# Long convolution of a conformer block: a timed schedule replaced by plain loops, with taps added on the matmul bank

## The chip, the cores and the metric

The kernel runs on one core of one Trainium2 chip. The metric is the device time of one execution in microseconds, as the median of several runs. Inside the core, TensorE (PE) does matmuls, VectorE (DVE), ScalarE (ACT) and GpSimdE (POOL) do elementwise work, and SyncE (SP) issues the weight loads. Each engine works through its own queue in the order in which the instructions were built into the program.

## The reference, cut to what matters

The whole program is a chain of blocks on a 256 x 1024 activation: a mixing layer, a cross-attention, a feed-forward layer, this conformer block, a feed-forward layer, a sparse attention and a last feed-forward layer. Only the conformer block is touched. The input h is a normalized x.

```python
def conformer_conv_module(h, w_in, b_in, w_dw, b_dw, ln_g, ln_b, w_out):
    a, g = jnp.split(h @ w_in + b_in, 2, axis=-1)
    u = a * jax.nn.sigmoid(g)
    u = lax.conv_general_dilated(          # 31 taps, depthwise, causal
        u, w_dw[:, None, :].astype(u.dtype), window_strides=(1,),
        padding=[(CONV_WIDTH - 1, 0)], dimension_numbers=('NWC', 'WIO', 'NWC'),
        feature_group_count=D_MODEL) + b_dw
    ...                                     # layer norm over the channels
    u = jax.nn.silu(uf).astype(h.dtype)
    return u @ w_out
```

## The kernel before, in words

Channels lie on the 128 partitions and the 256 positions along the free dimension, so the 1024 channels make eight tiles, m = 0 to 7. For each tile, the block first forms the product of w_in with x (`product_of`): two blocks of 128 channels in one bank, the value and the gate. For m = 1 and 2 the weights are split in a high and a low half (`mm3`, three matmuls for each of 16 pairs, L215 to L217); for m = 3 to 7 raw weights meet `cxg` (L990). DVE multiplies the bank by a broadcast of 1/rms (`rb`, L971 and L973), ACT applies tanh and a bias (L975, L976; below "the pair"), and DVE combines them (L977) to u(m), the tile `cu`.

The convolution adds 31 shifted copies of u(m), each scaled by a weight for each channel. Three engines share them. PE takes `CONV_PE[m]` of the shortest shifts as matmuls with a diagonal matrix `cdg` made by ACT (L1042, L1048), into a bank `bt`. POOL takes the `CONV_GP[m]` longest: ACT writes each scaled copy to a `cpr` tile, of which there are four (L1028), and POOL adds them in `cyp` (L1029). DVE takes the rest with one instruction per tap, (u x weight) + y, in the SBUF tile `cy` (L1015). Then DVE adds the bank to cy (L1057), and POOL or DVE adds cyp (L1059). The mean of tile 0 is broadcast (`cb`) and taken off every tile as a first guess of the mean. ACT squares y, and PE sums y and its square over the channels into `zb` (L1077). Behind the last tile follow the statistics, the normalization, silu, the split into two halves `yy`, and the product with c_out.

The order of the work is set by the table `CONF_AT`: `timed` starts each unit ("in" for the gated product, "pe", "gp", "dv", "fin", and "x") at its listed time and lets it take turns. What this gives each engine is a fixed queue. The unit "x" runs the generator `rest`, which multiplies the residual x by its gain and 1/rms in place (L438, eight instructions, behind a broadcast `bc_x1`).

Weights are loaded through a ring of four raw tiles `wraw` (L181). ACT casts a half (L198), and the rest is a subtraction (L200) on DVE, or for c_out chunks above the first on POOL.

Of the kernel before, what the change touches and what calls it, by code (L numbers as in the profile page):

```python
# [103 lines left out]
class Net:  # L104
# [825 lines left out]
    def conformer(self, first, pool):  # L930
# [6 lines left out]
        rb = zb = cb = None  # L937
        bt, yp = [None] * KT, [None] * KT
        have = set()

        def need(*keys):
            while not have.issuperset(keys):
                yield
# [13 lines left out]
        for m in range(KT):
            nc.vector.tensor_scalar(xg[:, m, :], self.x[:, m, :], gg[:, m : m + 1], None, op0=ALU.mult)

        def inp(m):  # L960
            nonlocal rb, zb
            b = b0
            if m:
                b, pb = product_of(m)
            yield
# [12 lines left out]
            have.add(f"u{m}")  # L978

        def product_of(m):  # L980
            nonlocal rb, zb
            w = self.chunk("c_in", m, **({"stop": "c_out"} if m < KT - 1 else {"room": 2}))
            pb = self.bank()
            b = [pb[:, 0:S], pb[:, S : 2 * S]]
            raw = [r.rearrange("p (k c) -> p k c", k=4) for r in w] if m >= CONV_N3 else None

            def product(i, k):
                c = slice(i * P, i * P + P)
                if raw:
                    nc.tensor.matmul(b[i][:, 0:S], raw[k // 4][:, k % 4, c], xg[:, k, :],  # L990
                                     start=(k == 0), stop=(k == KT - 1))
                else:
                    self.mm3(b[i][:, 0:S], w[k][:, :, c], self.xx[:, k], k == 0, k == KT - 1)

            for i in range(2):
                for k in range(KT):
                    product(i, k)
                if m == 1 and i == 0:
                    rb = self.bcast(r12, "x")
                    zb = self.zbank(2 * NT)  # L1000
            return b, pb

        def dv(m):
            yield from need(f"u{m}")
            y, u = ys[m], us[m]
            if m > 2:
                yield from need("c")
                nc.scalar.activation(y, cb, AF.Identity, bias=self.col("c_b", m), scale=-1.0)  # L1010
                nc.vector.scalar_tensor_tensor(y, u, tap(m, 0), y, op0=ALU.mult, op1=ALU.add)
            else:
                nc.vector.tensor_scalar(y, u, tap(m, 0), self.col("c_b", m), op0=ALU.mult, op1=ALU.add)
            for t in range(1 + CONV_PE[m], W - CONV_GP[m]):
                nc.vector.scalar_tensor_tensor(y[:, t:S], u[:, 0 : S - t], tap(m, t), y[:, t:S], op0=ALU.mult, op1=ALU.add)  # L1015
                if t % 4 == 0:
                    yield
            have.add(f"d{m}")
            yield
# [622 lines left out]
```

## Time and profile before

| | |
|---|---|
| median of 3 runs | 1132.01 us (1129.48 to 1132.69) |
| profiled execution | 1132.2 us |
| span of its trace | 1130.4 us |
| PE busy | 1070.3 us (95%) |
| DVE busy | 827.4 us (73%) |
| ACT busy | 638.2 us (56%) |
| POOL busy | 195.4 us (17%) |
| granted TensorE clock, mean | 0.974 |

The span runs from the first to the last instruction of the trace; busy time is the time in which an engine had an instruction at work. These are means over stages with different limits. In the timelines a row gives the start in us, the length of the group, the engine, the source line, the operation with output and inputs, and the count; in square brackets stands how long the engine was idle before it and what ended that. Instructions of one engine overlap by some 0.08 us, so a group's length divided by its count is the spacing. [...]

### The profile page before, as it was taken

The numbers are of one execution on the slowest core, as the hardware profiler recorded it, in microseconds if no ns is written. First come the engines' busy times: TensorE is split into PE (matmuls) and PEld (weight loads), VectorE is DVE, ScalarE is ACT, GpSimd is POOL, SyncE is SP. The second block draws the span as 40 slices with busy tenths as digits, with TensorE's granted clock in tenths as the row PEclk, the third lists the DMA queues.
The fourth block names the chain that finished last, engine by engine and source line by source line (L and its number), as shares of the span: only waits on it lengthen the run. The fifth ranks groups of instructions, "written<-read, shape, count | busy, mean of one in ns | idle before, by whom it ended". The sixth has DMA issues, their size and how long they took to land.

```text
span 1130.4 us, 19501 instructions
## 1 busy us (share of the span) xinstructions
PE 1070.3 (95%) x7282; PEld 984.6 (87%) x7282; DVE 827.4 (73%) x1654; ACT 638.2 (56%) x1231; POOL 195.4 (17%) x388
## 2 busy tenths in 40 slices
...
GB/s 233 220 167 158 127 147 155 128 135 191 187 193 178 219 169 71 65 85 93 75 113 176 190 191 183 223 173 189 95 112 189 18 76 149 188 190 192 179 208 31
DMA packets 52439, 171.38 MB, mean 152 GB/s; under 512 B 8440, under 2 KB 10360, under 8 KB 52344
## 3 DMA queue, kind: packets, MB, share of 16 engines
...
HBM read 169.07 MB, written 1.05 MB: 150 GB/s over the span
## 4 chain that ended last, share of the span: by engine, by line
PE 79%; DVE 12%; ACT 3%; issue 2%; DMA 2%; POOL 1%; SPq 0%; POOLq 0%; ACTq 0%; DVEq 0%
PE pb L223 28%; PE pb L224 14%; PE pb L215 9%; PE pb L216 9%; PE pb L217 9%; DVE cy L1015 5%; DMA wraw<-in_w_in_dram 1%; ACT wpr L198 1%; DVE wpr L200 1%; DVE xx L278 1%; DVE xres L438 1%; DVE xres L395 1%; PE bh L1254 1%; DMA wraw<-in_n_out_dram 1%; PE zb L376 1%
## 5 line engine op out<-in xcount | busy, mean ns | idle before, releaser
L200 DVE TENSOR_TENSOR wpr<-wraw,wpr 128x1024 fp32r<-128x1024 f32 (+1 forms) x298 | 361.1, 1214 | 178.7 <-ACT wpr L198 176.4
L198 ACT CAST wpr<-wraw 128x1024 fp32r<-128x1024 f32 (+1 forms) x304 | 313.4, 1033 | 203.1 <-PE pb L224 96.0
L223 PE MATMUL pb<-xx,wpr 128*128 128x512 f32 x840 | 294.3, 393 | 0.0
L224 PE MATMUL pb<-xx,wpr 128*128 128x256 f32 x840 | 235.5, 280 | 0.0
L223 PEld LDWEIGHTS pb<-xx,wpr 128*128 128x128 f32 x840 | 158.5, 189 | 34.0
L223 PE MATMUL pb<-fhs,wpr 128*128 128x512 f32 x528 | 186.0, 394 | 0.0
L224 PEld LDWEIGHTS pb<-xx,wpr 128*128 128x128 f32 x840 | 158.5, 189 | 0.0
L224 PE MATMUL pb<-fhs,wpr 128*128 128x256 f32 x528 | 147.3, 279 | 0.0
L215 PE MATMUL pb<-xx,wpr 128*128 128x256 f32 x456 | 129.7, 287 | 7.7 <-ACT xx L277 7.7
L216 PE MATMUL pb<-xx,wpr 128*128 128x256 f32 x456 | 130.4, 287 | 2.5 <-DVE xx L278 2.5
L217 PE MATMUL pb<-xx,wpr 128*128 128x256 f32 x456 | 128.9, 283 | 0.0
L223 PEld LDWEIGHTS pb<-fhs,wpr 128*128 128x128 f32 x528 | 99.0, 187 | 23.0
L224 PEld LDWEIGHTS pb<-fhs,wpr 128*128 128x128 f32 x528 | 99.0, 188 | 0.0
L215 PEld LDWEIGHTS pb<-xx,wpr 128*128 128x128 f32 x456 | 86.7, 192 | 9.4 <-ACT xx L277 8.0
L216 PEld LDWEIGHTS pb<-xx,wpr 128*128 128x128 f32 x456 | 87.3, 191 | 4.2 <-DVE xx L278 3.3
L217 PEld LDWEIGHTS pb<-xx,wpr 128*128 128x128 f32 x456 | 87.4, 192 | 0.0
L215 PE MATMUL pb<-yy,wpr 128*128 128x256 f32 x256 | 73.1, 288 | 2.3 <-ACT yy L282 2.3
L216 PE MATMUL pb<-yy,wpr 128*128 128x256 f32 x256 | 72.7, 284 | 0.0
L217 PE MATMUL pb<-yy,wpr 128*128 128x256 f32 x256 | 72.6, 284 | 0.0
L1015 DVE SCALAR_TENSOR_TENSOR cy<-cu,cwh,cy 128x238 f32<-128x238 f32 (+18 forms) x117 | 71.6, 669 | 0.1
L869 ACT COPY ft<-pb 128x256 f32<-128x256 f32 x105 | 38.5, 368 | 55.2 <-PE pb L224 55.2
L1029 POOL TENSOR_TENSOR cyp<-cyp,cpr 128x229 f32<-128x229 f32 (+11 forms) x70 | 59.9, 860 | 26.1 <-ACT cpr L1028 22.0
...
## 6 DMA issues: line engine op xcount, KB each, us to landing
wraw<-in_up_dram SPq DMA_DIRECT2D x44, 512.0 KB, 4.0
wraw<-in_up2a_dram SPq DMA_DIRECT2D x44, 512.0 KB, 4.4
wraw<-in_up2b_dram SPq DMA_DIRECT2D x44, 512.0 KB, 3.8
wraw<-in_w_in_dram SPq DMA_DIRECT2D x22, 512.0 KB, 4.6
wraw<-in_n_in_dram SPq DMA_DIRECT2D x20, 512.0 KB, 4.1
wraw<-in_wkv_dram SPq DMA_DIRECT2D x16, 512.0 KB, 3.7
wraw<-in_dn_dram SPq DMA_DIRECT2D x16, 512.0 KB, 4.4
wraw<-in_c_in_dram SPq DMA_DIRECT2D x16, 512.0 KB, 4.1
```

Source lines behind the costliest of these rows:

```text
L198: self.nc.scalar.copy(hi, raws[j])
L200: lane.tensor_tensor(lo, raws[j], hi.bitcast(F32), op=ALU.subtract)
L215: mm(out, left[:, 0], right[:, 0], start=start, stop=False, skip_group_check=True)
L216: mm(out, left[:, 0], right[:, 1], start=False, stop=False, skip_group_check=True)
L217: mm(out, left[:, 1], right[:, 0], start=False, stop=stop, skip_group_check=True)
L223: mm(out, left[:, 0], right, start=start, stop=False, skip_group_check=True)
L224: mm(out[:, 0], left[:, 1], right[:, 0], start=False, stop=stop, skip_group_check=True)
L278: nc.vector.scalar_tensor_tensor(lo, src, g, hi.bitcast(F32), op0=ALU.mult, op1=ALU.subtract)
L376: self.nc.tensor.matmul(zb[:, tt : tt + 1], src[:, tt * P : tt * P + P], self.ones, start=(src is acc), stop=(src is sq))
L869: nc.scalar.copy(t, b[:, 1])
L1015: nc.vector.scalar_tensor_tensor(y[:, t:S], u[:, 0 : S - t], tap(m, t), y[:, t:S], op0=ALU.mult, op1=ALU.add)
L1029: nc.gpsimd.tensor_tensor(y[:, t:S], y[:, t:S], pr[:, t:S], op=ALU.add)
```

## The change

The schedule table is gone. A plain loop issues, tile by tile, the product of the next tile, its gate, its diagonal matmuls and its POOL taps, and then the DVE taps and the end of the current tile. DVE's taps add in place on the bank `bt` behind the diagonal matmuls, and one DVE add then brings the bank to `cy`. POOL adds straight on `cy`, which ACT has set up with the bias (and tap 0 for m up to 2; for the others tap 0 is POOL's). There is no `cyp`. The numbers of taps change: PE 45 to 38 in all, DVE 117 and the eight of tap 0 to 113, POOL 70 adds to 94. The diagonal tiles have 12 buffers where they had 24. The subtractions for c_out are all DVE's. The second step of `rest`, the rescaling of x, is called behind the product with c_out.

```diff
-CONV_PE = [4, 1, 1, 4, 1, 15, 11, 8]
-CONV_GP = [8, 10, 10, 10, 14, 6, 9, 11]
+CONV_PE = [4, 3, 3, 3, 4, 5, 6, 10]
+CONV_GP = [13, 13, 12, 12, 12, 11, 9, 7]
...
-        lane = self.nc.gpsimd if name == "c_out" and idx > 0 else self.nc.vector
-        lane.tensor_tensor(lo, raws[j], hi.bitcast(F32), op=ALU.subtract)
+        self.nc.vector.tensor_tensor(lo, raws[j], hi.bitcast(F32), op=ALU.subtract)
...
+        def pe(m):
+            bt[m] = self.bank("bt")
+            n = CONV_PE[m]
+            for t in range(1, n + 1):
+                d = pool.tile([P, P], F32, name="cdg", tag="cdg", bufs=12)
+                nc.scalar.mul(d, self.ident, tap(m, t))
+                nc.tensor.matmul(bt[m][:, t:S], d, us[m][:, 0 : S - t], start=(t == 1), stop=(t == n))
 
         def dv(m):
...
+            b, u = bt[m], us[m]
+            for t in range(1 + CONV_PE[m], W - CONV_GP[m]):
+                nc.vector.scalar_tensor_tensor(b[:, t:S], u[:, 0 : S - t], tap(m, t), b[:, t:S], op0=ALU.mult, op1=ALU.add)
+
+        def gp(m):
             y, u = ys[m], us[m]
+            shifts = list(range(W - CONV_GP[m], W))
             if m > 2:
...
+                shifts = [0] + shifts
             else:
...
+                nc.scalar.activation(y, u, AF.Identity, bias=self.col("c_b", m), scale=tap(m, 0))
+            for t in shifts:
                 pr = pool.tile([P, S], F32, name="cpr", tag="cpr", bufs=4)
                 nc.scalar.mul(pr[:, t:S], u[:, 0 : S - t], tap(m, t))
                 nc.gpsimd.tensor_tensor(y[:, t:S], y[:, t:S], pr[:, t:S], op=ALU.add)
...
-        timed([(u[0], u[1], kinds[u[2]](*u[3:])) for u in CONF_AT])
+        gated(0, None)
+        pe(0)
+        gp(0)
+        next(rest)
+        for m in range(KT):
+            if m + 1 < KT:
+                gated(m + 1, product(m + 1))
+                pe(m + 1)
+                gp(m + 1)
+            if m == 0:
+                for k in range(KT):
+                    nc.vector.tensor_scalar(xg[:, k, :], self.x[:, k, :], gg[:, k : k + 1], None, op0=ALU.mult)
+            dv(m)
+            fin(m)
...
         acc = self.proj("c_out")
+        next(rest)
```

The numbers of the lines shift, too: the DVE tap L1015 becomes L979, the add of the bank L1057 becomes L997, the product by rb L973 becomes L959, u's L977 becomes L963, the diagonal matmul L1048 becomes L974, the raw product L990 becomes L948, the sums L1077 become L1010, the copies L1028 become L991, the rescaling L438 becomes L425, and the cast L198 becomes L186.

The builder orders the instructions of each engine. On DVE, in the piece where tile 1 ends and tile 2 goes on, these rows stood before (`cy1`, `cy2` are the sums of tiles 1 and 2, `bt` a bank, `cag` the gate's tile):

```order
L1015 SCALAR_TENSOR_TENSOR cy1_5160<-cu1_5152,cwh_5168,cy1_5160 128x238
L1015 SCALAR_TENSOR_TENSOR cy2_5161<-cu2_5153,cwh_5168,cy2_5161 128x253
L1015 SCALAR_TENSOR_TENSOR cy1_5160<-cu1_5152,cwh_5168,cy1_5160 128x237
L1015 SCALAR_TENSOR_TENSOR cy2_5161<-cu2_5153,cwh_5168,cy2_5161 128x252
L1015 SCALAR_TENSOR_TENSOR cy1_5160<-cu1_5152,cwh_5168,cy1_5160 128x236
L1015 SCALAR_TENSOR_TENSOR cy2_5161<-cu2_5153,cwh_5168,cy2_5161 128x251
L1057 TENSOR_TENSOR cy1_5160<-bt_5378,cy1_5160 128x255
L1015 SCALAR_TENSOR_TENSOR cy2_5161<-cu2_5153,cwh_5168,cy2_5161 128x250
L973 TENSOR_TENSOR cag_5475<-pb_5411,bc_x_5208 128x512
L1015 SCALAR_TENSOR_TENSOR cy2_5161<-cu2_5153,cwh_5168,cy2_5161 128x249
```

Now a single tile's taps follow one another; here is a piece of tile 0 (`bt_5185` its bank, `xres` the residual x):

```order
L979 SCALAR_TENSOR_TENSOR bt_5185<-cu0_5151,cwh_5168,bt_5185 128x244
L425 SCALAR_TENSOR_TENSOR xres_67<-xres_67,par_68,bc_x1_5256 128x256
L979 SCALAR_TENSOR_TENSOR bt_5185<-cu0_5151,cwh_5168,bt_5185 128x243
L425 SCALAR_TENSOR_TENSOR xres_67<-xres_67,par_68,bc_x1_5256 128x256
L979 SCALAR_TENSOR_TENSOR bt_5185<-cu0_5151,cwh_5168,bt_5185 128x242
L425 SCALAR_TENSOR_TENSOR xres_67<-xres_67,par_68,bc_x1_5256 128x256
L959 TENSOR_TENSOR cag_5307<-pb_5258,bc_x_5175 128x512
L979 SCALAR_TENSOR_TENSOR bt_5185<-cu0_5151,cwh_5168,bt_5185 128x241
L425 SCALAR_TENSOR_TENSOR xres_67<-xres_67,par_68,bc_x1_5256 128x256
L979 SCALAR_TENSOR_TENSOR bt_5185<-cu0_5151,cwh_5168,bt_5185 128x240
L963 SCALAR_TENSOR_TENSOR cu1_5152<-cag_5307 128x256
```

Two sums went forward in turn; now all taps of a tile stand in one chain on its bank, with the next tile's `cag` and `cu` between the last ones. The rescaling of x (L425), which stood in one block behind all other taps, now stands among the taps of tiles 0 and 1, although the source calls it last.

On PE, before, the product of tile 3, the start of that of tile 4 and two diagonal taps stood like this (`pb` is a product's bank, and each product row stands for four matmuls):

```order
L1048 MATMUL bt_5378<-cu1_5152,cdg_5376 128x255
L990 MATMUL pb_5411<-cxg_5167,wraw_4979 128x256 x4
L990 MATMUL pb_5411<-cxg_5167,wraw_5046 128x256 x4
L990 MATMUL pb_5411<-cxg_5167,wraw_4979 128x256 x4
L990 MATMUL pb_5411<-cxg_5167,wraw_5046 128x256 x4
L1048 MATMUL bt_5461<-cu2_5153,cdg_5448 128x255
L990 MATMUL pb_5484<-cxg_5167,wraw_5051 128x256 x4
L990 MATMUL pb_5484<-cxg_5167,wraw_5056 128x256 x4
```

Now, ahead of the product of tile 5 (`pb_5725`), with `zb` the sums and `sq` the square of a tile:

```order
L1010 MATMUL zb_5177<-ones_71,cy3_5162 128x1
L974 MATMUL bt_5646<-cu4_5155,cdg_5647 128x255
L974 MATMUL bt_5646<-cu4_5155,cdg_5650 128x254
L974 MATMUL bt_5646<-cu4_5155,cdg_5653 128x253
L974 MATMUL bt_5646<-cu4_5155,cdg_5656 128x252
L1010 MATMUL zb_5177<-ones_71,sq_5715 128x1
L1010 MATMUL zb_5177<-ones_71,cy3_5162 128x1
L1010 MATMUL zb_5177<-ones_71,sq_5715 128x1
L948 MATMUL pb_5725<-cxg_5167,wraw_5620 128x256 x4
L948 MATMUL pb_5725<-cxg_5167,wraw_5622 128x256 x4
```

Product 5 now stands behind four diagonal taps of tile 4 and the sums of tile 3; before, the whole of products 3 and 4 had a single diagonal tap ahead of each.

On ACT, near the end of the loop, before (the copies for POOL of tile 7, a diagonal matrix of its, and the casts of c_out's halves, `wpr`):

```order
L1042 ACTIVATE cdg_5954<-ident_69,cwh_5168 128x128
L1028 ACTIVATE cpr_5956<-cu7_5158,cwh_5168 128x231
L1028 ACTIVATE cpr_5959<-cu7_5158,cwh_5168 128x230
L1028 ACTIVATE cpr_5962<-cu7_5158,cwh_5168 128x229
L1028 ACTIVATE cpr_5965<-cu7_5158,cwh_5168 128x228
L1028 ACTIVATE cpr_5995<-cu7_5158,cwh_5168 128x227
L1028 ACTIVATE cpr_5998<-cu7_5158,cwh_5168 128x226
L198 CAST wpr_6122<-wraw_5737 128x1024
L198 CAST wpr_6127<-wraw_6113 128x1024
L198 CAST wpr_6132<-wraw_6115 128x1024
```

Now, behind the last copies of tile 6:

```order
L991 ACTIVATE cpr_5894<-cu6_5157,cwh_5168 128x226
L186 CAST wpr_5927<-wraw_5920 128x1024
L973 ACTIVATE cdg_5973<-ident_69,cwh_5168 128x128
L973 ACTIVATE cdg_5976<-ident_69,cwh_5168 128x128
L973 ACTIVATE cdg_5979<-ident_69,cwh_5168 128x128
L973 ACTIVATE cdg_5982<-ident_69,cwh_5168 128x128
L186 CAST wpr_6127<-wraw_5925 128x1024
L186 CAST wpr_6132<-wraw_5930 128x1024
L961 ACTIVATE cag_5949<-cag_5949,cbh_5170 128x256
L962 ACTIVATE cag_5949<-cag_5949,par_68 128x256
L186 CAST wpr_6137<-wraw_6123 128x1024
L991 ACTIVATE cpr_5986<-cu7_5158,cwh_5168 128x256
```

Three casts now stand ahead of the pair of tile 7 (L961 and L962 on `cag_5949`), and one more ahead of the first copy of tile 7; before, the pair of tile 7 was long done there.

## Rows read from the trace of the kernel before

**Rows 1.** The first line of the page.
```profile
span 1130.4 us, 19501 instructions
```

**Rows 2.** Busy by stretch: length, PE, PEld, DVE, ACT, POOL, PE clock, DMA.
```profile
441.06:449.06 8.00, 7.47 (x62) 7.30 (x62) 5.71 (x27) 5.73 (x19) 3.99 (x15) 1.00 0.00 0
449.06:530.00 80.94, 66.96 (x315) 58.67 (x314) 80.26 (x134) 49.91 (x123) 56.20 (x67) 0.89 0.26 85
441.06:566.16 125.10, 88.56 (x425) 77.82 (x424) 112.45 (x216) 68.15 (x168) 83.57 (x99) 0.80 0.22 72
```

**Rows 3.** The chain of waits near the end of the stage: start, duration, what.
```profile
555.60 0.41 DVE cy L1059
...
566.16 1.01 PE pb L215 x3
```

**Rows 4.** Timeline of DVE: start, time of the group, engine, line, operation.
```profile
451.01 15.30 DVE L1015 SCALAR_TENSOR_TENSOR cy<-cu,cwh,cy 128x250 f32<-128x250 f32 x23
466.23 0.68 DVE L973 TENSOR_TENSOR cag<-pb,bc_x 128x512 f32<-128x512 f32 x1
...
467.96 0.41 DVE L977 SCALAR_TENSOR_TENSOR cu<-cag 128x256 f32<-128x256 f32 x1
...
527.47 6.53 DVE L1015 SCALAR_TENSOR_TENSOR cy<-cu,cwh,cy 128x236 f32<-128x236 f32 x17
...
543.32 11.85 DVE L438 SCALAR_TENSOR_TENSOR xres<-xres,par,bc_x 128x256 f32<-128x256 f32 x8 [3.05 <-ACT bc_x L330]
```

**Rows 5.** Timeline of POOL in the stage; in brackets idle time before.
```profile
450.24 12.73 POOL L1029 TENSOR_TENSOR cyp<-cyp,cpr 128x232 f32<-128x232 f32 x16 [4.04 <-ACT cpr L1028]
...
492.92 0.69 POOL L1029 TENSOR_TENSOR cyp<-cyp,cpr 128x238 f32<-128x238 f32 x1 [3.51 <-ACT cpr L1028]
493.57 0.86 POOL L1059 TENSOR_TENSOR cy<-cyp,cy 128x235 f32<-128x235 f32 x1
```

**Rows 6.** Timeline of PE in the stage.
```profile
452.18 0.28 PE L216 MATMUL pb<-xx,wpr 128*128 128x256 f32 x1
452.30 0.28 PE L217 MATMUL pb<-xx,wpr 128*128 128x256 f32 x1
...
499.98 2.30 PE L1048 MATMUL bt<-cu,cdg 128*128 128x255 f32 x10
502.12 0.28 PE L1077 MATMUL zb<-ones,cy 128*128 128x1 f32 x2
...
503.82 7.15 PE L990 MATMUL pb<-cxg,wraw 128*128 128x256 f32 x32
...
526.92 3.72 PE L1048 MATMUL bt<-cu,cdg 128*128 128x255 f32 x8 [2.90 <-DVE cu L977]
```

**Rows 7.** Durations by line: ns minimum, median, maximum.
```profile
L502 DVE SCALAR_TENSOR_TENSOR aqT<-pb,par,bc_x x4: 469/470/478, 31.0 to 33.5; 128x256 f32<-128x256 f32 x4
...
L890 DVE SCALAR_TENSOR_TENSOR fg<-fu,par,fg x44: 474/484/486, 260.2 to 370.1; 128x256 f32<-128x256 f32 x44
...
L973 DVE TENSOR_TENSOR cag<-pb,bc_x x7: 676/677/680, 447.6 to 523.9; 128x512 f32<-128x512 f32 x7
```

**Rows 8.** Timeline of DVE in an earlier stage.
```profile
283.87 1.00 DVE L890 SCALAR_TENSOR_TENSOR fg<-fu,par,fg 128x256 f32<-128x256 f32 x2 [0.19 <-ACT fg L888]
```

**Rows 9.** Timeline of ACT in the stage.
```profile
468.80 1.61 ACT L1028 ACTIVATE cpr<-cu,cwh 128x234 f32<-128x234 f32 x4
...
540.10 2.92 ACT L198 CAST wpr<-wraw 128x1024 fp32r<-128x1024 f32 x3
```

**Rows 10.** DMA issues: KB each, median us to landing.
```profile
wraw<-in_c_out_dram SPq DMA_DIRECT2D x8, 512.0 KB, 4.3
```

**Rows 11.** Stretches with the clock granted to PE.
```profile
33.00:36.00 3.00, 0.58 (x6) 0.37 (x4) 3.00 (x7) 1.77 (x4) 1.10 (x2) 1.00 0.82 276
468.00:471.00 3.00, 2.57 (x6) 2.13 (x7) 3.00 (x9) 2.42 (x7) 1.64 (x1) 0.50 0.01 3
...
526.00:530.00 4.00, 3.08 (x7) 2.52 (x8) 4.00 (x12) 2.68 (x8) 2.25 (x1) 0.53 0.00 0
```

More of the change, by code (lines that the diff above doesn't have):

```diff
@@ L45 @@
     (4.681, 1, "v", 2), (4.986, 1, "v", 3), (5.392, 0.56, "out")]
-CONF_AT = [
[10 rows of a table removed]
-    (19.392, 0.476, "fin", 7)]
 NSA_AT = [
@@ L936, in conformer @@
         b0, (r12, rest, gg) = first
[L937 to L943, printed above, removed]
+        bt, cb = [None] * KT, None
         def tap(m, t):
@@ L955, in conformer, with product, gated @@
         nc.gpsimd.tensor_scalar(bh, self.par[:, o : o + KT], 0.5, None, op0=ALU.mult)
[L957 to L965, printed above, removed]
+        rb = self.bcast(r12, "x")
+        zb = self.zbank(2 * NT)
+        def product(m):
+            w = self.chunk("c_in", m, **({"stop": "c_out"} if m < KT - 1 else {"room": 2}))
+            pb = self.bank()
+            raw = [r.rearrange("p (k c) -> p k c", k=4) for r in w] if m >= CONV_N3 else None
+            for i in range(2):
+                b, c = pb[:, i * S : i * S + S], slice(i * P, i * P + P)
+                for k in range(KT):
+                    if raw:
+                        nc.tensor.matmul(b, raw[k // 4][:, k % 4, c], xg[:, k, :], start=(k == 0), stop=(k == KT - 1))
+                    else:
+                        self.mm3(b, w[k][:, :, c], self.xx[:, k], k == 0, k == KT - 1)
+            return pb
+        def gated(m, pb):
             ag = pool.tile([P, 2, S], F32, name="cag", tag="cag", bufs=2)
             if m == 0:
-                while rb is None:
-                    yield
                 for i in range(2):
-                    nc.vector.tensor_tensor(ag[:, i, :], b[i][:, 0:S], rb, op=ALU.mult)
+                    nc.vector.tensor_tensor(ag[:, i, :], b0[i][:, 0:S], rb, op=ALU.mult)
             else:
@@ L977, in inp @@
             nc.vector.scalar_tensor_tensor(us[m], ag[:, 1, :], 1.0, ag[:, 0, :], op0=ALU.add, op1=ALU.mult)
[L978 to L1001, printed above, removed]
+        def pe(m):
[5 more added lines that the diff above has]
+                nc.tensor.matmul(bt[m][:, t:S], d, us[m][:, 0 : S - t], start=(t == 1), stop=(t == n))
@@ L1012, in dv @@
             else:
[L1013 to L1019, printed above, removed]
-        def gp(m):
-            yield from need(f"u{m}")
-            u, t0 = us[m], W - CONV_GP[m]
-            y = yp[m] = pool.tile([P, S], F32, name="cyp", tag="cyp", bufs=4)
-            nc.scalar.mul(y[:, t0:S], u[:, 0 : S - t0], tap(m, t0))
-            for t in range(t0 + 1, W):
+                nc.scalar.activation(y, u, AF.Identity, bias=self.col("c_b", m), scale=tap(m, 0))
@@ L1029, in gp @@
                 nc.gpsimd.tensor_tensor(y[:, t:S], y[:, t:S], pr[:, t:S], op=ALU.add)
-                if t % 4 == 0:
-                    yield
-            have.add(f"g{m}")
-            yield
-        def pe(m):
-            yield from need(f"u{m}")
-            n = CONV_PE[m]
-            for c in range(0, n, 4):
-                dg = []
-                for t in range(c + 1, min(c + 4, n) + 1):
-                    d = pool.tile([P, P], F32, name="cdg", tag="cdg", bufs=24)
-                    nc.scalar.mul(d, self.ident, tap(m, t))
-                    dg.append(d)
-                yield
-                if c == 0:
-                    bt[m] = self.bank("bt")
-                for t, d in enumerate(dg, c + 1):
-                    nc.tensor.matmul(bt[m][:, t:S], d, us[m][:, 0 : S - t], start=(t == 1), stop=(t == n))
-            have.add(f"p{m}")
-            yield
         def fin(m):
             nonlocal cb
-            yield from need(f"d{m}", f"p{m}")
-            y, t0 = ys[m], W - CONV_GP[m]
-            if CONV_PE[m]:
-                nc.vector.tensor_tensor(y[:, 1:S], bt[m][:, 1:S], y[:, 1:S], op=ALU.add)
-            yield from need(f"g{m}")
-            (nc.gpsimd if m < KT - 2 else nc.vector).tensor_tensor(y[:, t0:S], yp[m][:, t0:S], y[:, t0:S], op=ALU.add)
+            y = ys[m]
+            nc.vector.tensor_tensor(y[:, 1:S], bt[m][:, 1:S], y[:, 1:S], op=ALU.add)
             if m == 0:
```

14 lines of the change are left out of this document (1 added, 13 removed), and 10 rows, old and new, of the table CONF_AT.

## The prediction

> **What bounds the kernel now.** The page first, for the size: the span is 1130.4 us [rows 1], the profiled execution took 1132.2 and the median of the runs is 1132.01, so a sum made against this one execution stands for the median too. The edit touches only the conformer stage, so the stretches come next: from its first DVE statistic at 441.06 to the first c_out matmul at 566.16 it takes 125.10 us, and in 449.06 to 530 DVE is busy 80.26 of 80.94 us while PE has 66.96 and POOL 56.20 [rows 2]. DVE sets the pace there. Third, the timelines, to see what this busy time is made of. With POOL adding beside them, 23 taps take 15.30 us, 0.665 each; 17 taps in a later row take 6.53, 0.384 each [rows 4]. POOL shows the same from its side: 16 adds in 12.73 us, 0.80 each, against 0.65 from one add's start to the next start when it is undisturbed [rows 5]. The two slow each other down. The DVE instruction that reads a matmul's bank, L973, does not show it: 676 to 680 ns in all seven places, though POOL was adding in some of them [rows 7]. Last, the chain at the end of the stage. PE gets the last gated tile, u7, at 526.92 [rows 6]; the last DVE add ends at 556.0 [rows 3], 29 us later, and 11.85 us of that are the eight rescalings of x, L438 [rows 4]. From 556.0 to 566.16 is a tail of 10.15 us that the change leaves as it is.
>
> **The change, costed.** *One tap.* 113 taps now add in place on the bank, where 117 stood in SBUF. No row writes a bank this way. Reading one costs nothing: L502 with a bank as source takes 470 ns, L890 with SBUF alone 484 [rows 7]. The taps of one tile now form a single chain, each on the result of the one ahead; two dependent L890 take 1.00 us, so the second starts 0.52 after the first [rows 8], while the 0.384 belongs to two chains in turn. I take 0.50, with 0.384 and 0.665 (the contended SBUF tap) as its bounds. [...] *One POOL add.* 94 in place of 70; I take 0.69, near the undisturbed 0.65, with 0.80 as the bound.
>
> *The order.* Before, PE had the next product queued ahead of, or beside, several tiles' work. Now each tile makes a lap: u(m) is ready, PE does the diagonal taps of m and then product(m+1), DVE multiplies it by rb, ACT does the pair, DVE makes u(m+1). PE is a queue, so product(m+1) stands behind diag(m), which waits for u(m): the 2.1 us from the start of L973 at 466.23 to the end of cu at 468.37 [rows 4] is PE idle in each lap, where before it had other matmuls. So I add up laps. Prices: a diagonal tap 0.43 at full clock (five in the rows from 499.98 to 502.12) of two records each, and 0.88 at half (twice 0.43, and four in 3.72); zb sums of one tile 0.85 (two in 502.12 to 503.82); a product of 32 rows 7.1; a split matmul 0.12, so 5.7 for 48 [all rows 6]. ACT's cpr 0.40, its cast of a weight half 1.0 [rows 9]. A hand-off between engines 0.2 and the ACT pair 0.9 (estimates: 2.14 less 0.68 and 0.41 of the DVE rows leaves 1.05).
>
> - To u0: 8.0, as before [rows 2].
> - Lap 0: four diagonal taps at half clock 3.4 (PE has nothing while the first broadcast is awaited), two broadcasts 0.6 by estimate, split product 5.7, 2.1, hand-offs 0.6: 12.4.
> - Lap 1: the zb sums of y0 stand inside product 2 and wait for POOL, whose subtraction of the mean stands behind 13 adds of tile 1: 1.0 start, 13 x 0.69 = 9.0, 0.8, then 16 matmuls 1.9, zb 0.85, 2.1, 0.5: 16.2.
> - Lap 2: the square of y1 stands behind twelve cprs on ACT, which go at POOL's pace (four buffers): 1.6 + 8 x 0.69 + 0.8, rest of the zb sums 0.65, rest of product 3 2.65, 2.1, 0.4: 13.7.
> - Laps 3, 4, 5 are PE's own: diag 1.3, 1.7, 2.15, zb 0.85, product 7.1, 2.1: 11.35, 11.75, 12.2. DVE needs 1.5 until the diagonal taps are in, 14 x 0.50, and 2.4 from L973 to cu, 10.9 in all, and is hidden, narrowly.
> - Lap 6: four c_out casts now stand on ACT ahead of pair 7, and the raw loads wait for slots that DVE's subtractions free. Square and cast 1.4, first cpr 0.4, six adds 4.1, last cpr 0.4, cast 1.0, DVE's subtraction 1.2, load 4.3 [rows 10], cast 1.0, pair 0.9, cu 0.4, eight hand-offs 1.6: 16.7. The subtraction's 1.2 is an estimate from ACT's 1.0 for the same half. Before, five of these halves were POOL's.
> - Lap 7: ten diagonal taps at half clock 8.8 (PE idled in lap 6), then 13 taps 6.5 and the add on y 0.4: 15.7.
> - Tail: 10.15.
>
> The sum is 128.15, against 125.1: +3. Seen whole: u7 comes 102 us into the stage where it came at 86, and what follows it shrinks from 29 to 16. The rescaling of x leaves the end, but not for where the source puts it: in the built order the eight stand among DVE's taps of tiles 0 and 1, where lap 1 waits for POOL; were DVE the bound there, 8 x 0.48 = 4 us would be back. The 24 to 12 diagonal buffers cost nothing as long as ACT makes them a lap ahead.
>
> **The rivals.** *The clock falls in every lap.* Behind a pause of 2.90 us PE resumes at half rate: the granted clock is 0.53 in 526 to 530; in 468 to 471, after a longer pause, it is 0.50 for the three microseconds that follow the restart, 1.5 us of matmul lost [rows 6, 11]. Each lap has a pause of 2.1 to 2.6. Against it: a pause of about 2.4 in 33 to 36 left the clock at 1.00 [rows 11]. Six laps at 1.5 to 2.4 add 9 to 14: 1144 to 1149. [...]
>
> *Taps on a bank are dear.* At 0.63, DVE's share of a lap is 12.7 and replaces PE's in laps 3 to 5, and lap 7 grows by 1.7: about +5, so 1140. At 0.665 to 0.81 (the latter a tap at POOL's contended pace) it is up to +16: 1151. It decides from about 0.53 on. Speaking against it: L502.
>
> *No lap but PE's own (the other side).* If POOL and ACT keep ahead of PE in laps 1, 2 and 6, each takes about 11.35 and 4.85 + 2.35 + 5.35 = 12.5 come off: 1122.5. DVE at 99% before and slowed by POOL [rows 2, 4] speaks for it: once that is gone, nothing else of the stage is full. It decides when these three laps lose more than 6.5 together. With a cheaper lap 7, too (full clock, 4.5 less), it is 1118.
>
> *The stage moves by less than can be told*: a later part absorbs it. No row shows slack behind the tail; I give it little.
>
> **Numbers.** A change under 0.3% (3.4 us) can't be told from none here. The forecast holds 0.46: 1135, its own range 1130 to 1140, half of it inside the 0.3%. Clock 0.20, dear taps 0.10, the faster rival 0.19, no change 0.05. Faster 0.19; same 0.23 + 0.05 = 0.28; slower 0.23 + 0.30 = 0.53. For the range the lower end at 1121 leaves out the far end of the faster rival, about 0.08, and the upper at 1150 the far ends of the other two, about 0.08.
>
> **What would show it.** Right: L979 near 0.50 from start to start with no spread beside POOL, POOL's adds at 0.65 to 0.69; u(m) to u(m+1) of 11 to 12 us in laps 3 to 5, 14 to 17 in laps 1, 2 and 6; PE waiting on DVE's cu once a lap; the last tap ending some 118 us after the first statistic; the L425 rescalings between taps of tiles 0 and 1. Wrong: a granted clock of 0.5 in laps 3 to 5; L979 over 0.53; pair 7 not waiting for a cast, or lap 1 not waiting for POOL.

## The result, and the profile after

The changed kernel takes 1144.76 us (median; 1142.62 to 1146.31 in four runs), beside 1132.30 for the kernel before (median of four runs here): ratio 1.0114, 95% interval 1.0088 to 1.0141. It is slower by 12.5 us, and the forecast of 1135 was 10 short. The profiled execution took 1142.62, the quickest of the four, with a span of 1140.8, 10.4 more than before [rows 1]. From the first statistic at 441.19 to the first c_out matmul at 576.62 the stage now takes 135.4 where it took 125.1 [rows 2]: the stage holds the whole difference, and what follows it is as long as before.

From the page after: the first line, busy time by engine, and the groups of POOL's adds and DVE's taps (busy us, mean ns, idle before and its releaser).

```profile
span 1140.8 us, 19527 instructions
...
PE 1075.5 (94%) x7268; PEld 987.0 (87%) x7268; DVE 804.7 (71%) x1646; ACT 647.1 (57%) x1243; POOL 183.1 (16%) x400
...
L992 POOL TENSOR_TENSOR cy<-cy,cpr 128x231 f32<-128x231 f32 (+13 forms) x94 | 67.2, 715 | 32.1 <-ACT cpr L991 25.4
...
L979 DVE SCALAR_TENSOR_TENSOR bt<-cu,cwh,bt 128x245 f32<-128x245 f32 (+18 forms) x113 | 53.6, 475 | 20.7 <-PE bt L974 17.6
```

The 113 taps cost 53.6 us of DVE, and DVE now waits 17.6 us for diagonal banks. The place to read the result is the lap, from the end of one cu to the end of the next. The windows below are the head, laps 0 to 7, the tail and the whole stage; then come four stretches of PE in and behind its pauses. Columns as in [rows 2], with the count of instructions behind each busy time; the PE clock is the granted part of the full clock.

```profile
441.19:448.82 7.63, 1.73 (x8) 1.25 (x7) 5.04 (x26) 4.78 (x15) 3.92 (x15) 0.70 0.00 0
448.82:462.22 13.40, 10.81 (x60) 9.92 (x60) 8.54 (x20) 8.75 (x21) 9.01 (x13) 0.79 0.00 1
462.22:481.71 19.49, 11.93 (x70) 11.20 (x70) 9.92 (x25) 10.86 (x26) 9.77 (x14) 0.74 0.01 1
481.71:495.89 14.18, 11.24 (x46) 9.23 (x46) 9.40 (x20) 8.11 (x19) 9.18 (x14) 0.88 0.16 50
495.89:508.01 12.12, 9.66 (x48) 8.33 (x48) 8.56 (x19) 8.35 (x20) 9.43 (x14) 1.00 0.26 79
508.01:523.17 15.16, 13.43 (x50) 11.12 (x49) 8.13 (x18) 8.35 (x21) 8.83 (x13) 0.77 0.22 73
523.17:535.29 12.12, 10.35 (x51) 8.86 (x51) 8.01 (x17) 8.25 (x21) 8.13 (x12) 1.00 0.28 88
535.29:551.57 16.28, 11.99 (x50) 10.04 (x50) 11.50 (x20) 10.95 (x21) 8.26 (x10) 0.85 0.48 173
551.57:567.83 16.26, 7.87 (x28) 6.62 (x28) 12.37 (x21) 5.86 (x12) 6.96 (x8) 0.71 0.43 141
567.83:576.63 8.80, 4.34 (x17) 3.67 (x17) 6.54 (x29) 2.61 (x7) 0.00 (x0) 0.50 0.00 1
441.19:576.63 135.44, 93.36 (x425) 80.24 (x424) 88.01 (x207) 76.88 (x180) 73.50 (x112) 0.80 0.20 66
...
494.00:496.50 2.50, 0.00 (x0) 0.00 (x0) 1.73 (x4) 0.91 (x2) 0.99 (x1) 1.00 0.80 264
...
505.80:507.70 1.90, 0.09 (x2) 0.00 (x1) 1.55 (x4) 0.93 (x3) 1.31 (x2) 1.00 0.86 250
...
509.50:516.00 6.50, 6.50 (x20) 5.45 (x19) 4.69 (x10) 4.54 (x11) 5.87 (x9) 0.50 0.04 13
...
536.70:539.60 2.90, 2.90 (x8) 2.30 (x8) 0.64 (x1) 2.04 (x6) 2.67 (x4) 0.50 0.40 137
```

No engine is full in any of these laps: DVE has 88.01 of 135.44 us, where it had 112.45 of 125.10 before. What is long are laps 1, 4, 6 and 7. PE's timeline says what ended its idle time (in brackets):

```profile
453.49 0.41 PE L203 MATMUL pb<-xx,wpr 128*128 128x256 f32 x1
...
462.28 1.55 PE L974 MATMUL bt<-cu,cdg 128*128 128x255 f32 x6 [2.60 <-DVE cu L963]
...
474.09 0.59 PE L1010 MATMUL zb<-ones,cy 128*128 128x1 f32 x2 [5.06 <-POOL cy L1006]
...
474.90 0.41 PE L202 MATMUL pb<-xx,wpr 128*128 128x256 f32 x1
...
496.53 0.38 PE L1010 MATMUL zb<-ones,cy 128*128 128x1 f32 x2 [2.76 <-POOL cy L1006]
...
498.73 7.15 PE L948 MATMUL pb<-cxg,wraw 128*128 128x256 f32 x32
...
508.16 2.79 PE L974 MATMUL bt<-cu,cdg 128*128 128x255 f32 x8
...
511.89 9.15 PE L948 MATMUL pb<-cxg,wraw 128*128 128x256 f32 x32
...
551.62 1.64 PE L974 MATMUL bt<-cu,cdg 128*128 128x255 f32 x3 [4.34 <-DVE cu L963]
```

In lap 1 PE stands for 5.06 us until POOL has taken the mean off y0 (473.31 to 474.03, behind its 13 adds for tile 1), and finishes product 2 at half clock: a split matmul begins 0.21 behind the last, where 0.12 was priced. In lap 4 PE pauses for 1.8 us, resumes, and the clock then falls while it is working: 0.50 from 509.5 to 516.0, through most of product 5, which takes 9.15 against 7.15. Lap 6 ends as forecast, with pair 7 behind a cast that waits for its load. Two timelines to it, of POOL in lap 0 and of ACT in lap 6:

```profile
449.92 9.95 POOL L992 TENSOR_TENSOR cy<-cy,cpr 128x238 f32<-128x238 f32 x13 [3.66 <-ACT cpr L991]
```

```profile
548.93 1.04 ACT L186 CAST wpr<-wraw 128x1024 fp32r<-128x1024 f32 x1 [3.67 <-DMA wraw<-in_c_out_dram]
549.88 0.51 ACT L961 ACTIVATE cag<-cag,cbh 128x256 f32<-128x256 f32 x1
```

Thirteen adds on one y take 9.95 us (10.03 in lap 1), so 0.765 from one to the next; the forecast had 0.69.

### The profile page after: what moved, and what is told of

Its sections match the earlier page's. It is cut to its first block, busy times and chain, and to the rows that moved or that the text cites. A ratio compares the mean times of both kernels' runs of the same rounds, so it can differ in the third digit from the quotient of the medians.

```text
span 1140.8 us, 19527 instructions
## 1 busy us (share of the span) xinstructions
PE 1075.5 (94%) x7268; PEld 987.0 (87%) x7268; DVE 804.7 (71%) x1646; ACT 647.1 (57%) x1243; POOL 183.1 (16%) x400
## 4 chain that ended last, share of the span: by engine, by line
PE 81%; DVE 7%; POOL 5%; ACT 4%; issue 2%; DMA 2%; SPq 0%; POOLq 0%; ACTq 0%; DVEq 0%
PE pb L210 28%; PE pb L211 14%; PE pb L202 9%; PE pb L204 9%; PE pb L203 9%; POOL cy L992 3%; DVE bt L979 2%; ACT wpr L186 1%; PE pb L948 1%; DVE wpr L187 1%; DVE xx L265 1%; PE bt L974 1%; DVE xres L382 1%; PE bh L1195 1%; PE zb L1010 1%
## 5 line engine op out<-in xcount | busy, mean ns | idle before, releaser
L187 DVE TENSOR_TENSOR wpr<-wraw,wpr 128x1024 fp32r<-128x1024 f32 (+1 forms) x304 | 368.6, 1214 | 182.1 <-ACT wpr L186 179.8
L186 ACT CAST wpr<-wraw 128x1024 fp32r<-128x1024 f32 (+1 forms) x304 | 313.7, 1033 | 208.2 <-PE pb L211 93.6
L992 POOL TENSOR_TENSOR cy<-cy,cpr 128x231 f32<-128x231 f32 (+13 forms) x94 | 67.2, 715 | 32.1 <-ACT cpr L991 25.4
L979 DVE SCALAR_TENSOR_TENSOR bt<-cu,cwh,bt 128x245 f32<-128x245 f32 (+18 forms) x113 | 53.6, 475 | 20.7 <-PE bt L974 17.6
```

The costliest lines, as they stand in the source:

```text
L186: self.nc.scalar.copy(hi, raws[j])
L187: self.nc.vector.tensor_tensor(lo, raws[j], hi.bitcast(F32), op=ALU.subtract)
L979: nc.vector.scalar_tensor_tensor(b[:, t:S], u[:, 0 : S - t], tap(m, t), b[:, t:S], op0=ALU.mult, op1=ALU.add)
L992: nc.gpsimd.tensor_tensor(y[:, t:S], y[:, t:S], pr[:, t:S], op=ALU.add)
```

## The experiments

My theory after the result: the bank does what the forecast said, and the loss is the order, a product that PE can't begin until the diagonal taps of the tile ahead of it have their u. Rivals: the split of taps (POOL's 94), the clock, and the early rescaling of x. Each ratio below is to the kernel before, run on the same chip; its median was 1131.95 in the first four experiments, 1131.74 in the next four and 1132.29 in the last four.

**1. The product one tile further ahead of the diagonal taps.**

```diff
         gated(0, None)
+        pb = product(1)
         pe(0)
...
-                gated(m + 1, product(m + 1))
+                gated(m + 1, pb)
+                if m + 2 < KT:
+                    pb = product(m + 2)
                 pe(m + 1)
```

> Theory A (the laps are serial: product m+1 stands behind the diagonal taps of m, so PE idles while u(m+1) is made): with product m+2 issued ahead of the diagonal taps of m+1, u(m+1) no longer waits for PE; laps 3 to 5 fall from 12.1, 15.2 and 12.1 us to 10 to 11 (DVE: 14 taps at 0.51 and 2.4 for the gate), the fall of the clock in lap 4 goes, and the kernel gains 8 to 14 us, to 1131 to 1137. Rival B (DVE's single chain on the bank is the bound): laps stay at 11.5 to 12.5, gain under 4 us.

1121.47, ratio 0.9907 [0.9883, 0.993]: some 23 us under the kernel after, and faster than before. The stage takes 114.99. Its laps 1, 3 and 5 by stretches, and PE's timeline in lap 3:

```profile
458.89:469.52 10.63, 3.98 (x29) 3.48 (x28) 7.77 (x20) 8.40 (x21) 9.13 (x14) 0.91 0.01 2
...
485.63:495.56 9.93, 9.93 (x47) 8.75 (x47) 8.55 (x20) 7.64 (x19) 8.37 (x13) 1.00 0.38 121
...
507.74:516.99 9.25, 9.25 (x49) 8.27 (x47) 7.46 (x17) 7.42 (x17) 7.70 (x12) 1.00 0.34 103
```

```profile
485.43 7.15 PE L948 MATMUL pb<-cxg,wraw 128*128 128x256 f32 x32
492.42 1.45 PE L974 MATMUL bt<-cu,cdg 128*128 128x255 f32 x6
```

PE is busy 9.93 of 9.93 us in lap 3 and 9.25 of 9.25 in lap 5: the wait for cu that stood ahead of the diagonal taps is covered by the next product, up to tile 7, whose taps still wait 1.23. Laps 3 to 5 come to 31.4, where they took 39.4, although in lap 4 (12.18) PE waits 0.80 for POOL and the clock is at 0.86. The other gains are laps 0, 1 and 6. Product 1 stands ahead of the diagonal taps of tile 0, and lap 0 takes 10.46 for 13.40. Product 2 is done before its u is wanted, so lap 1 falls from 19.49 to 10.63, of which lap 2, in which PE begins product 3 only at 472.95, behind the column sum of y0, gives 1.9 back (16.11 for 14.18). Lap 6 takes 11.97 for 16.28, and lap 7 gives 1.7 back. The theory holds, and the order is worth more than I had put on it.

**2. Sixteen spare matmuls in PE's pause**, between product m+1 and the diagonal taps of m+1; they read x and write a bank that nothing reads.

```diff
...
+                fill = self.bank("fill")
+                for _ in range(16):
+                    nc.tensor.matmul(fill[:, 0:S], self.xx[:, 0, 0, 0:P], self.xx[:, 0, 0], start=True, stop=True)
...
```

> 16 matmuls whose result nobody reads, 1.9 us at full clock, stand between product m+1 and the diagonal taps of m+1. Theory A with the clock: the clock's falls in laps 4 and 6 go (3 us and 2 us), lap 1's stays, since its pause lies inside a product; the kernel gains 3 to 6 us, to 1139 to 1142. Rival (falls cost nothing of their own): no gain, or up to 2 us lost in laps where the fill runs at half clock.

1137.18, ratio 1.0052 [1.0031, 1.0073]: 7.6 less than after, with more work on PE. PE between laps 3 and 4:

```profile
504.53 2.25 PE L1022 MATMUL fill<-xx 128*128 128x256 f32 x16
...
507.06 1.98 PE L974 MATMUL bt<-cu,cdg 128*128 128x255 f32 x8
...
509.46 7.15 PE L948 MATMUL pb<-cxg,wraw 128*128 128x256 f32 x32
```

Lap 4 falls from 15.16 to 11.74, the forecast's 11.75, and the product is back at 7.15. Lap 1 stays at 19.5, as its pause lies inside product 2, where nothing was filled in. In the profiled executions the stage is 4.9 shorter than after (130.55 for 135.44), 3.4 of it in lap 4 and the rest in laps 6 and 7; that of experiment 1 is 20.4 shorter. So the clock alone is about a quarter of the difference between the kernel after and experiment 1, or a third by the medians (7.6 of 23).

**3. Nine POOL taps instead of 13, 13 and 12 for tiles 0 to 2; DVE takes the rest.**

```diff
-CONV_GP = [13, 13, 12, 12, 12, 11, 9, 7]
+CONV_GP = [9, 9, 9, 12, 12, 11, 9, 7]
```

> Nine POOL taps in place of 13, 13 and 12 for tiles 0 to 2, the rest to DVE. Theory A: lap 1, where PE waits 5.06 us for POOL and then runs at half clock, falls from 19.5 to 14 or 15 us; lap 2 about unchanged (POOL 3 us less, DVE 1.5 us more); the kernel gains 3 to 6 us. Rival (POOL is not on the path): DVE's 4 + 4 + 3 more taps cost up to 5 us.

1142.39, ratio 1.0092 [1.0059, 1.0124]: at most 2.4 gained on after, within what the runs scatter. A miss: POOL's wait did shrink, from 5.06 to 0.65, yet lap 1 became longer, 20.81. PE in lap 1:

```profile
467.10 0.98 PE L279 MATMUL zb<-ones,cy 128*128 128x1 f32 x4 [3.26 <-DVE cy L997]
...
471.06 0.58 PE L1010 MATMUL zb<-ones,cy 128*128 128x1 f32 x2 [0.65 <-POOL cy L1006]
```

DVE's chain of tile 0 is four taps longer, and seven rescalings of x stand in it, so the column sum of y0, which heads PE's lap, waits 3.26 for it; and behind that pause PE does product 2 at half clock, 0.41 a matmul up to 478.48. The wait went from POOL to DVE and took the clock with it. Lap 1 is not POOL's alone, as I had it: whoever was last, PE stood and then ran at half rate.

**4. The kernel after with DVE's taps in SBUF**: one copy of the bank into a tile, the same taps on that tile.

```diff
+            b = pool.tile([P, S], F32, name="cyd", tag="cyd", bufs=2)
+            nc.vector.tensor_scalar(b[:, 1:S], bt[m][:, 1:S], 1.0, None, op0=ALU.mult)
...
+            bt[m] = b
```

> The DVE taps add in an SBUF tile that starts as a copy of the bank; all else as in the changed kernel. If the bank is what keeps DVE and POOL apart: taps go from 0.51 to between 0.66 and 0.81 us beside POOL, POOL's adds from 0.765 to 0.80 or more, laps 3 to 5 grow by 2 to 4 us each, the kernel loses 10 to 20 us. Rival (the bank brings nothing): taps stay near 0.5, and the kernel loses only the copy, about 0.4 us a lap, 1 to 3 us.

1158.57, ratio 1.0248 [1.0215, 1.0281], 14 above after; eight copies of 0.42 are in it, and so is a lower clock (mean of the four runs 0.960, after 0.970). Durations of its taps (ns minimum, median, maximum):

```profile
L981 DVE SCALAR_TENSOR_TENSOR cyd<-cu,cwh,cyd x113: 451/474/924, 453.7 to 585.9; 128x245 f32<-128x245 f32 x8, 128x244 f32<-128x244 f32 x8, 128x243 f32<-128x243 f32 x8, 128x242 f32<-128x242 f32 x8
```

DVE's timeline, the first eight taps of tile 0, with SBUF:

```profile
453.71 6.45 DVE L981 SCALAR_TENSOR_TENSOR cyd<-cu,cwh,cyd 128x251 f32<-128x251 f32 x8
```

and of the kernel after:

```profile
452.73 4.09 DVE L979 SCALAR_TENSOR_TENSOR bt<-cu,cwh,bt 128x251 f32<-128x251 f32 x8 [3.91 <-PE bt L974]
```

Beside POOL's adds a tap takes 0.81 in SBUF and 0.51 on the bank; the medians are the same, 474 ns there and 476 here (458 to 484), but the longest is 924 there. From start to start, taps of one chain with no POOL instruction beside them are 0.50 apart in SBUF (thirteen in 6.50 us from 579.89) as on the bank (15 places); with one, eight are 0.80 apart in SBUF (from 453.71 on) and 74 places on the bank have a mean of 0.51. Here the bank took the contention away and added nothing of its own: the two medians and the two spacings of 0.50 agree.

**5. The kernel before, with only its taps moved onto the bank**: its table of units, its split and its order stay; a tile's taps wait for its diagonal matmuls.

```diff
-            yield from need(f"u{m}")
+            yield from need(f"u{m}", f"p{m}")
...
-                nc.vector.scalar_tensor_tensor(y[:, t:S], u[:, 0 : S - t], tap(m, t), y[:, t:S], op0=ALU.mult, op1=ALU.add)
+                b = bt[m]
+                nc.vector.scalar_tensor_tensor(b[:, t:S], u[:, 0 : S - t], tap(m, t), b[:, t:S], op0=ALU.mult, op1=ALU.add)
```

> The kernel before, its table of times and its split of taps kept, with DVE's taps on the bank (a tile's taps wait for its diagonal matmuls). Theory A (the bank takes the contention away, and the order of the plain loop gives more back): taps fall from 0.665 to 0.4 to 0.5 us beside POOL, POOL's adds to 0.77, and the kernel gains 6 to 18 us against the kernel before, to 1114 to 1126. Rival (under the old order the wait for the diagonal matmuls eats the gain): within 5 us of before.

1118.20, ratio 0.9875 [0.9854, 0.9896]: 13.5 faster than before, by this part of the change alone. From its page, POOL's adds:

```profile
L1030 POOL TENSOR_TENSOR cyp<-cyp,cpr 128x229 f32<-128x229 f32 (+11 forms) x70 | 49.8, 717 | 11.0 <-ACT cpr L1029 6.9
```

DVE's timeline, its longest run of taps:

```profile
459.07 12.98 DVE L1016 SCALAR_TENSOR_TENSOR bt<-cu,cwh,bt 128x250 f32<-128x250 f32 x34
```

POOL's adds fall from a mean of 860 ns to 717, and the 34 taps, on two tiles' banks in turn, take 0.382 each, with POOL adding beside them. That is also what the 17 taps in SBUF of the kernel before took [rows 4], but there POOL was held up. Its timeline before, during those 17 taps:

```profile
527.75 6.78 POOL L1029 TENSOR_TENSOR cyp<-cyp,cpr 128x235 f32<-128x235 f32 x1 [5.21 <-ACT cpr L1028]
```

That one add ended 0.5 behind the last of the taps; without it the mean before would be 774.

**6. The kernel before, with the rescaling of x early in its table.**

```diff
-    ... (11.907, 0.624, "x"), ...
+    ... (1.35, 0.624, "x"), ...
```

> The kernel before, with the unit of the rescaling started at 1.35 in place of 11.907, so that its eight instructions stand among the taps of tiles 0 and 1. If the 11.85 us at the end were the cost of the rescaling: a gain of 4 to 8 us (they cost DVE 4 to 6 us where they now stand). Rival (they filled a wait for POOL and for c_out's casts): gain under 2 us, or a loss of up to 4.

1132.78, ratio 1.0007 [0.9993, 1.0022]: no change. The eight rescalings leave the end, but there DVE then waits for POOL, as the add of one of the last partial sums shows (another, at 549.51, waits 2.71):

```profile
545.10 0.86 DVE L1059 TENSOR_TENSOR cy<-cyp,cy 128x234 f32<-128x234 f32 x1 [1.93 <-POOL cyp L1029]
```

The 11.85 us of rescaling at the end of the stage before [rows 4] only filled a wait.

**7. The kernel after, with c_out's subtractions from half 1 on given back to POOL.**

```diff
-        self.nc.vector.tensor_tensor(lo, raws[j], hi.bitcast(F32), op=ALU.subtract)
+        lane = self.nc.gpsimd if name == "c_out" and idx > 0 else self.nc.vector
+        lane.tensor_tensor(lo, raws[j], hi.bitcast(F32), op=ALU.subtract)
```

> The changed kernel, with c_out's subtractions above the first chunk on POOL as before. Theory A: a subtraction on POOL takes 2.5 us and stands behind POOL's adds, so lap 6 stays as long or grows by up to 3 us, lap 7 loses two subtractions of DVE (2.4 us): between a gain of 2 and a loss of 3. Rival (DVE's extra subtractions are what the change costs): a gain of 4 to 8 us.

1145.04, ratio 1.0117 [1.0094, 1.014]: no difference from after that can be told, with intervals of some 3 us to either side. In the profiled execution the laps differ (17.17 for 19.49 in lap 1, 15.47 for 12.12 in lap 3), so this holds for the total alone.

**8. Experiment 1 with twelve cpr buffers instead of four**, so that ACT needn't follow POOL.

```diff
-                pr = pool.tile([P, S], F32, name="cpr", tag="cpr", bufs=4)
+                pr = pool.tile([P, S], F32, name="cpr", tag="cpr", bufs=12)
```

> Product m+2 ahead as in the first experiment, and 12 buffers for the copies that ACT makes for POOL in place of 4. If ACT's pair of the next tile, queued behind copies that go at POOL's pace, is what is left in laps 1, 2 and 4: those laps lose 2 to 5 us each and the kernel gains 4 to 9 us on the first experiment, to 1112 to 1118. Rival (POOL's 13 adds at 0.765 set the lap): gain under 2.

1121.82, ratio 0.991 [0.9888, 0.9932]: no gain on experiment 1. u1 and u2 come earlier, at 457.08 and 464.52, but u3 at 487.57. POOL and PE there:

```profile
449.97 24.24 POOL L992 TENSOR_TENSOR cy<-cy,cpr 128x238 f32<-128x238 f32 x31 [3.68 <-ACT cpr L991]
```

```profile
474.94 0.58 PE L1010 MATMUL zb<-ones,cy 128*128 128x1 f32 x2 [4.23 <-POOL cy L1006]
```

POOL does 31 adds without a break, 0.78 each, and PE waits for its subtraction inside product 3 instead of product 2. It was POOL's pace, not ACT's buffers, that held the early laps.

**9. Experiment 5 with the new split** of taps.

```diff
-CONV_PE = [4, 1, 1, 4, 1, 15, 11, 8]
+CONV_PE = [4, 3, 3, 3, 4, 5, 6, 10]
-CONV_GP = [8, 10, 10, 10, 14, 6, 9, 11]
+CONV_GP = [13, 13, 12, 12, 12, 11, 9, 7]
```

> The fifth experiment (order of before, taps on the bank) with the changed kernel's numbers of taps for PE and POOL. If the order alone made the changed kernel slow, it stays within 5 us of the fifth experiment's 1118. Rival (the new split, with 13 POOL adds at 0.765 us in each tile where before had 8 to 14, is a large part): 1123 to 1135.

1124.00, ratio 0.9931 [0.991, 0.9953]: 5.8 above experiment 5. DVE's timeline where it makes u3:

```profile
475.80 0.42 DVE L977 SCALAR_TENSOR_TENSOR cu<-cag 128x256 f32<-128x256 f32 x1 [8.21 <-ACT cag L976]
```

DVE stands for 8.21 us, where in experiment 5 it stands for 0.17: ACT's pair is behind the copies that it makes at the pace of POOL's adds, more of them now.

**10. Experiment 5 with the rescaling of x early**.

```diff
-    ... (11.907, 0.624, "x"), ...
+    ... (1.35, 0.624, "x"), ...
```

> The fifth experiment with the rescaling started early as in the sixth. In the fifth the eight rescalings stand among the last taps and take some 4 us of DVE there; if DVE sets the end, 2 to 5 us are gained, to 1113 to 1116. Rival (POOL's copies and adds or c_out's casts set the end, as the sixth experiment suggests): no change within 2 us, or a loss.

1123.74, ratio 0.9929 [0.9914, 0.9945]: 5.5 above experiment 5, so with the taps on the bank the early place is a loss. DVE's timeline:

```profile
455.06 2.49 DVE L438 SCALAR_TENSOR_TENSOR xres<-xres,par,bc_x 128x256 f32<-128x256 f32 x3 [2.32 <-ACT bc_x L330]
...
461.93 0.50 DVE L977 SCALAR_TENSOR_TENSOR cu<-cag 128x256 f32<-128x256 f32 x1
```

The eight stand ahead of a cu in DVE's queue: it ends 13.8 us behind the first, where in experiment 5 it is 8.2 (450.96 to 459.15). The later tiles' u follow it.

**11. Experiment 1 with more diagonal taps on PE** in tiles 0 to 2, 6 and 7, and 24 diagonal buffers.

```diff
-CONV_PE = [4, 3, 3, 3, 4, 5, 6, 10]
+CONV_PE = [10, 8, 6, 3, 4, 5, 10, 14]
...
-                d = pool.tile([P, P], F32, name="cdg", tag="cdg", bufs=12)
+                d = pool.tile([P, P], F32, name="cdg", tag="cdg", bufs=24)
```

> The first experiment (product m+2 ahead) with more diagonal taps where PE waits for DVE: 10, 8 and 6 in tiles 0 to 2 in place of 4, 3, 3, and 10 and 14 in tiles 6 and 7 in place of 6 and 10; 24 diagonal buffers. DVE has 22 taps less, 11 us; if its taps set laps 1, 2 and the end, the kernel gains 4 to 8 us on the first experiment's 1121.5, to 1113 to 1117. Rival (ACT, with 22 more diagonal matrices at 0.3 us, or POOL sets these laps): 1119 to 1124.

1127.01, ratio 0.9954 [0.9937, 0.997]: 5.5 above experiment 1, a miss. Lap 1 takes 12.62 for 10.63 and lap 3 13.11 for 9.93. The cu that ends lap 1, on DVE's timeline, and what ACT does ahead of its pair:

```profile
471.93 0.43 DVE L963 SCALAR_TENSOR_TENSOR cu<-cag 128x256 f32<-128x256 f32 x1 [3.92 <-ACT cag L962]
```

```profile
468.96 2.14 ACT L973 ACTIVATE cdg<-ident,cwh 128x128 f32<-128x128 f32 x7
```

Each diagonal tap is also a diagonal matrix for ACT to make, and the pair stands behind them: seven here, where two take 0.68 at this place in experiment 1. In lap 3 nine are made ahead of the pair, where experiment 1 makes one.

**12. The kernel after, with POOL's adds of a tile on two partial sums in turn**, joined by a last add; there are as many adds as before.

```diff
...
+                a = y2 if i % 2 and t >= t0 else y
...
-                nc.gpsimd.tensor_tensor(y[:, t:S], y[:, t:S], pr[:, t:S], op=ALU.add)
+                nc.gpsimd.tensor_tensor(a[:, t:S], a[:, t:S], pr[:, t:S], op=ALU.add)
+            nc.gpsimd.tensor_tensor(y[:, t0:S], y[:, t0:S], y2[:, t0:S], op=ALU.add)
```

> The changed kernel with POOL adding by turns in two tiles, joined by a last add; 13 adds for tile 0 as before. If an add on the tile that the add ahead has just written costs more than an add on another tile: the spacing falls from 0.765 to about 0.65, lap 1 loses 1 to 2 us, and the kernel 2 to 5 us, to 1139 to 1143. Rival (0.765 is an add's own time here, or DVE's): spacing stays at 0.76, the kernel stays at 1144 to 1147.

1142.30, ratio 1.0093 [1.0078, 1.0108]: 2.5 less than after, less than the intervals can part. POOL's timeline:

```profile
452.21 0.68 POOL L996 TENSOR_TENSOR cyq<-cyq,cpr 128x236 f32<-128x236 f32 x1
452.85 0.68 POOL L996 TENSOR_TENSOR cy<-cy,cpr 128x235 f32<-128x235 f32 x1
```

From start to start 0.64, where the adds of one chain are 0.765 apart: an add that needs the one ahead of it costs 0.12 more. Lap 1 is 1.5 us shorter. The clock's fall moved to another lap here (product 4 takes 9.13), so the total says little of the 0.12. Two stretches of this execution, columns as in [rows 2]:

```profile
496.50:503.20 6.70, 6.70 (x20) 5.60 (x19) 4.50 (x10) 5.80 (x15) 6.24 (x10) 0.50 0.01 3
...
510.10:522.34 12.24, 10.39 (x51) 8.88 (x51) 8.54 (x18) 8.55 (x21) 8.39 (x13) 1.00 0.29 97
```

The fall comes behind a pause of 2.76, as long as the one ahead of lap 3 in the kernel after, which left the clock at 1.00; and behind a pause of 1.69, like the one of 1.81 ahead of the fall in the kernel after, there is none.

## Why the prediction was right or wrong

**The sign and the mechanism** came out: slower, and by the order of PE's queue. In one line by medians: before 1132; taps on the bank alone 1118 (experiment 5); with the new split too 1124 (9); with the plain order as well, which also moves c_out's subtractions (worth nothing by 7) and x (5.5 on experiment 5, by 10), 1145 (after). The last step also moves tap 0 to ACT and POOL, drops `cyp` and halves the diagonal buffers, which no run separates. So the bank gave 13.5, the split took back 6 and the plain loop 21; experiment 1, by issuing each product earlier, wins back 23, as much as the plain loop took and a little more. The forecast had bank, split and order inside one sum, +3 in all where +10.3 came; what that sum lacked follows point by point.

The time itself, 1144.76, lies outside the forecast's own 1130 to 1140 and inside the clock rival's 1144 to 1149. That rival had 0.20, and it is what made the difference: matmuls at half rate that the sum had at full rate come to some 0.9 us in lap 0, 2.8 in lap 1 and 3.2 in lap 4, nearly as much as the whole miss of 7.3; the other misses about cancel. One of the signs that the forecast named for being wrong, a clock of 0.5 in laps 3 to 5, was seen in lap 4; of the others, no tap is over 0.53, pair 7 does wait for a cast and lap 1 for POOL. The last tap ends 126 us after the first statistic, not 118.

**The tap, 0.50.** Right: 458 to 484 ns in all 113 places, 0.51 from start to start in a chain, with no spread beside POOL. The rival of dear taps falls: no run shows the 0.63 that it put on a tap on the bank, and the longest took 484 ns here and 493 in experiment 5. The row behind the lower bound of 0.384 is not one without POOL: during those 17 taps one POOL add, begun 0.28 behind the first of them, lasted 6.78 us (experiment 5). The bound itself stands, as taps of two chains with no POOL work beside them were 0.37 to 0.39 apart in that trace.

**The POOL add, 0.69.** Mis-sized: 0.765. I read it from an add at 492.92 whose follower writes another tile [rows 5]; in y's chain each waits for the last. It is 1.0 of lap 1's miss.

**Lap 1, 16.2 for 19.49.** The wait for POOL was forecast; what was not is the half rate behind it. Sixteen split matmuls at 0.21 and the zb sums cost 5.5 (474.09 to 479.6) where 2.75 was put. That is 2.8; with POOL's 1.0, and without the 0.5 put for hand-offs, it is the 3.3.

**Lap 0, 12.4 for 13.40.** Product 1 took 6.6 (453.13 to 459.69) where 5.7 was put, as its first matmuls went at half rate (0.41 each). No row stood behind the 0.6 for two broadcasts; the trace has one there, which took 0.71 (452.42 to 453.13). The pause of 2.60 ahead of the diagonal taps is no miss: the sum had 2.1 and 0.6 for hand-offs.

**Lap 3, 11.35 for 12.12.** The zb sums of y2 head PE's queue and wait for POOL's subtraction, 0.99 from 495.48, which waits for DVE's add on y2, 494.98: PE begins 0.64 behind the start of the lap. I had it begin at once.

**Lap 4, 11.75 for 15.16.** This is the rival that the clock falls, in one lap. Experiment 2 ties it to the pause: with the pause filled, the lap is 11.74. Of the four pauses ahead of laps 3 to 6 the first, with 2.8 us the longest, and the third left the clock at 1.00; behind the second and the fourth it fell. The forecast's rival had a fall in every lap and its likeliest case none in laps 3 to 6; two falls in four, which happened, stood nowhere. The length of the pause alone doesn't decide, as experiment 12 shows.

**Lap 2, lap 5, lap 6, lap 7.** 14.18 for 13.7, 12.12 for 12.2, 16.28 for 16.7 and 16.26 for 15.7. Lap 6 ended as told, by a cast that waited for its load, then the pair, then PE behind 4.34 us of pause. In lap 7 the two halves of the estimate were off against each other: the diagonal taps were quicker (7.1 for 8.8), and DVE then began its thirteen taps only at 560.76, behind two subtractions of c_out.

**Head and tail.** 7.63 for 8.0, and 8.80 for 10.15. "A tail of 10.15 us that the change leaves as it is" was wrong by 1.35: the steps of the reciprocal root share DVE with eight subtractions of the mean from y, of which six ran ahead of its last step before and three do now, and PE waits 1.81 for it where it waited 3.12.

**The sum.** The misses, -0.4, 1.0, 3.3, 0.5, 0.8, 3.4, -0.1, -0.4, 0.55 and -1.35, make 7.3, which is 135.4 less 128.15. Lap 1 and lap 4 are 6.7 of it, and most of that is matmuls at half rate.

**The rescaling of x.** It stood among DVE's taps of tiles 0 and 1, between 457.5 and 466, as told; that the early place costs nothing there was not tested on the kernel after. Its trace shows some 0.3 us in lap 0: product 1 ends at 459.69, and the product by rb begins only at 460.07, behind a rescaling, where in laps 1 and 2 it begins 0.04 behind the last matmul. In experiment 3, where DVE's chain of tile 0 set lap 1, seven rescalings stood in that chain. "The rescaling of x leaves the end" was taken for part of the gain (29 us shrinking to 16); experiment 6 shows that on the kernel before it is worth nothing.

**The faster rival** named 1122.5 if no lap but PE's own set the pace. The kernel after is far from it, and experiment 1 is at 1121.5 by another way: PE's wait, which the rival kept at 2.1 in each lap, is covered in most laps.
